# Attention values as two scaled 2-byte numbers instead of three, and the high part of the probabilities on ScalarE

## The chip, the core and the metric

The kernel runs on one NeuronCore of one Trainium2 chip. The metric is the time of one execution on the device in microseconds (us). A core has five engines that each work through a queue of their own in order: TensorE (PE, matrix products; PEld is its loading of weights), VectorE (DVE), ScalarE (ACT), GpSimd (POOL) and SyncE (SP, which here only issues DMAs). PE writes to eight PSUM banks of 128 x 512 fp32; the other operands lie in SBUF.

## The reference

One layer of an encoder on 1024 tokens of width 1024. After a normalisation, `x @ W_in` gives queries, keys and values for two attentions and two gates. Branch A is attention over a neighbourhood in a 2-D grid (8 heads, each with its own keys and values); branch B is attention over a sliding window (8 query heads that share 2 heads of keys and values). The gated branches go through `W_out`, and a SwiGLU block follows.

```python
p = jax.nn.softmax(s + bias[None], axis=-1)
o = jnp.einsum('brjhqk,brjkhd->brjqhd', p.astype(v.dtype), vg)
...
e = jnp.exp(s - m)
p = e / (jnp.sum(e, axis=-1, keepdims=True) + jnp.exp(sk - m))
o = jnp.einsum('bnkgqs,bnskd->bnqkgd', p.astype(v.dtype), vw)
...
x = x + jnp.einsum('btd,de->bte', y, w_out[l])
...
u = jax.nn.silu(jnp.einsum('btd,df->btf', h, w_gate[l])) * jnp.einsum('btd,df->btf', h, w_up[l])
x = x + jnp.einsum('btf,fd->btd', u, w_down[l])
```

All of it is fp32. On PE a product is made of parts: an fp32 operand is split into a high and a low part, and two or three matmuls stand for one product.

## The kernel before

The program has three stages: an opening (loads, splits, the projection of the first group of heads), the attention stage, and the long tail of branch products, `W_out` and the SwiGLU block. The change is in the first two.

**Groups and steps.** `order` (line 27) lists six groups: four "na" groups of two heads of branch A and two "sw" groups of four heads of branch B, in the order na 0, sw 0, na 1, sw 1, na 2, na 3. A head has eight blocks of 128 queries. One (head, block) is a step, so there are 16 steps in an na group, 32 in an sw group and 128 in all. The tiles of a group carry its number first (`o1_0_0` belongs to group 1, head 0 of it).

**One step** (`scores`, lines 679 to 710): two matmuls give the scores of 128 queries against up to 384 keys (L687, L688); DVE adds the bias and finds the bound (L693); ACT takes the exponential and its sum (L699); DVE and POOL make the scale 32768/sum (L701, L702); POOL writes the high fp16 part of the scaled probabilities `F` (L706) and DVE the low part (L707, which reads what L706 wrote); a DMA transpose on SP's queue puts both parts into `flipped` (L710). The tiles E, nm and F have 3, 4 and 3 buffers.

**Values** (`values`, lines 727 to 749) run LP = 6 steps behind the scores. A head has ten blocks: two of 128, four of 256 and four of 384 columns. The values `v` are kept as three bf16 parts of 64 columns each, and a block takes three matmuls (L745): parts 1 and 2 (128 columns of weights) with the high plane of the probabilities, the same two with the low plane, and part 3 (64 columns of weights) with the high plane. `store_half` (L718, L720) scales the finished half of a head by 1/32768.

**Projections.** While group g is in its steps, PE also works on the projection of group g+1 (`projection`, lines 252 to 481): eight tiles of 128 tokens, each 8 x 3 matmuls of 384 columns (L345) into a bank `pj` (three banks), given out in 64 pieces between the steps by `plan` (line 818). PE's order is written out by hand this way; the order on the other engines is set by a scheduler, but for the opening, where program order holds. `squares` and `scalings` normalise queries and keys (L358, L359, L363, L367, L408); `keys` and `pair` transpose them (L322, L315) and lay them out (L293, L294, L308, L309). `values_out` (lines 376 to 403) makes the three parts of the values: ACT the first (L385), DVE the rest (L399), POOL the second and third (`thirds`, L373, L374). In an sw group the values go through DRAM first, and the three parts are made at its end (`done`, L331 to L338).

**The opening.** Group 0 is projected by halves of four tiles. In the second half (`c` = 1), after k = 2, ACT squares the rows and `finish` runs for the first half. After half of k = 5 PE makes the keys' transposes (L322) into the bank `o`, of which there is one, and which until then holds tile 3 of the first half (`pj0_3`). The values of tiles 4 to 7 follow after k = 7, and then the projection of group 1.

## Time and profile before

| what | value |
|---|---|
| runs of the kernel before | 1350.4, 1354.04 and 3319.11 us (median 1354.04) |
| profiled execution, its own time | 1352.82 us |
| its span, first to last instruction | 1351.0 us |
| PE busy | 1325.9 us (98%) |
| DVE, ACT, POOL busy | 1040.8, 648.9, 257.1 us |
| L745, the matmuls of the values | 480, 101.9 us busy |
| first and last of them start at | 82.1 and 431.3 us |

The page gives the busy time of each engine, a chain of waits followed back from the last instruction, and groups of instructions with their count, their busy time, the mean duration of one, and the idle time of the engine ahead of them with what ended it. Matmuls overlap in the pipeline, so the duration of one is not what it costs; the distance from one start to the next is, and the timeline gives it. In a table by stretches, each engine's busy time stands with the count of its instructions, then PE's granted clock as a share of full speed, and the mean busy share of the 16 DMA engines.

### The profile page before, as it was taken

Reading aid. Unit: us, or ns where it says so; the run is one execution under the profiler, and the core shown is the slowest. Engines: PE = TensorE matmul, PEld = TensorE weight load, DVE = VectorE, ACT = ScalarE, POOL = GpSimd, SP = SyncE. Lnnn points to the kernel's source line nnn. Section 1 sums busy time; section 2 is a strip of 40 time slices with the busy share of each in tenths; the row PEclk is TensorE's granted clock in tenths of the full one; section 3 lists DMA queues with packets and bytes.
Section 4 is the critical chain, followed back from the end, with each engine's and each line's share of the span. In section 5 each row is a group of like instructions: output and inputs, shape, how many; then the busy total and the mean of one; then the engine's idle time right before and its main releaser. Section 6 shows DMA issues by size and latency. Waiting matters only on the chain.

```text
span 1351.0 us, 19529 instructions
## 1 busy us (share of the span) xinstructions
PE 1325.9 (98%) x6391; PEld 1085.3 (80%) x6391; DVE 1040.8 (77%) x2030; ACT 648.9 (48%) x1330; POOL 257.1 (19%) x581
## 2 busy tenths in 40 slices
...
GB/s 348 96 134 129 144 161 140 125 155 154 139 196 167 158 110 161 335 171 260 154 321 157 179 86 111 98 96 110 117 117 110 89 164 223 241 255 73 164 133 86
DMA packets 183338, 215.00 MB, mean 159 GB/s; under 512 B 110483, under 2 KB 113043, under 8 KB 183235
## 3 DMA queue, kind: packets, MB, share of 16 engines
...
## 4 chain that ended last, share of the span: by engine, by line
PE 89%; DMA 5%; DVE 2%; issue 1%; POOL 1%; ACT 1%; SPq 1%; DVEq 0%; ACTq 0%; POOLq 0%
PE pj L345 11%; PE bankZ L928 6%; PE bankZ L930 6%; PE bankZ L929 6%; PE bankY L928 6%; PE bankY L929 6%; PE bankY L930 6%; PE o L745 5%; PE bankX L928 5%; PE bankX L930 5%; PE bankX L929 5%; PE bankV L928 3%; PE bankV L929 3%; PE bankV L930 3%; PE pb L498 2%; PE pb L499 2%
## 5 line engine op out<-in xcount | busy, mean ns | idle before, releaser
L699 ACT ACTIVATE E<-E,nm 128x384 f32<-128x384 f32 (+3 forms) x128 | 75.4, 589 | 107.3 <-DVE nm L693 85.8
L745 PE MATMUL o<-flipped,v 128*128 128x256 f16 (+5 forms) x480 | 101.9, 297 | 10.2 <-DMA flipped<-F 9.0
L707 DVE SCALAR_TENSOR_TENSOR F<-E,nm,F 128x384 f16<-128x384 f32 (+1 forms) x128 | 85.7, 677 | 29.6 <-POOL F L706 29.2
L745 PEld LDWEIGHTS <-v 128*128 128x128 bf16 (+1 forms) x480 | 36.9, 101 | 72.7 <-issue 61.3
L706 POOL TENSOR_SCALAR F<-E,nm 128x384 f16<-128x384 f32 (+1 forms) x128 | 78.7, 617 | 34.8 <-DMA flipped<-F 21.0
L63 ACT CAST f<-f 128x512 fp32r<-128x512 f32 x87 | 51.7, 621 | 28.3 <-DMA f<-u_dram 27.7
L64 DVE TENSOR_TENSOR f<-f 128x512 fp32r<-128x512 f32 x87 | 56.5, 686 | 8.4 <-ACT f L63 8.2
L1334 POOL TENSOR_TENSOR rs<-rs,mhalf 128x4 f32<-128x4 f32 x2 | 2.1, 1077 | 318.0 <-DVE rs L1333 318.0
L367 POOL TENSOR_TENSOR ss<-ss,mhalf 128x4 f32<-128x4 f32 (+2 forms) x42 | 51.5, 1226 | 1.4
L693 DVE CUSTOM_DVE_ANT_0 E<-s,bna 128x384 f32<-128x384 f32 (+1 forms) x64 | 33.1, 520 | 22.6 <-PE s L688 20.0
L687 PE MATMUL s<-k,q 128*128 128x384 f32 (+1 forms) x128 | 44.4, 347 | 3.5 <-DVE nm L693 3.4
L693 DVE CUSTOM_DVE_ANT_0 E<-s,bsw,cols 128x384 f32<-128x384 f32 (+1 forms) x64 | 36.8, 577 | 6.9 <-PE s L688 5.5
L688 PE MATMUL s<-k,q 128*128 128x384 f32 (+1 forms) x128 | 41.5, 324 | 0.0
L702 POOL TENSOR_SCALAR nm<-nm 128x1 f32<-128x1 f32 x128 | 30.8, 244 | 38.9 <-DVE nm L701 33.1
L1344 ACT ACTIVATE u<-u 128x512 f32<-128x512 f32 x44 | 27.6, 630 | 19.4 <-DVE u L1343 18.8
L345 PE MATMUL pj<-wg_6h,h 128*128 128x384 f32 x96 | 33.7, 359 | 1.3 <-ACT wg_6h L63 1.3
L932 ACT COPY bankZ<-bankY 128x512 f32<-128x512 f32 x42 | 24.1, 575 | 22.3 <-PE bankY L930 22.3
L928 PE MATMUL bankY<-f,f_6h 128*128 128x512 f32 x88 | 34.4, 391 | 0.0
L929 PE MATMUL bankV<-f,f_5h 128*128 128x512 f32 x88 | 34.4, 391 | 0.0
L928 PE MATMUL bankV<-f,f_5h 128*128 128x512 f32 x88 | 34.4, 391 | 0.0
L928 PE MATMUL bankZ<-f,f_4h 128*128 128x512 f32 x88 | 34.3, 390 | 0.0
L929 PE MATMUL bankZ<-f,f_4h 128*128 128x512 f32 x88 | 34.3, 390 | 0.0
...
## 6 DMA issues: line engine op xcount, KB each, us to landing
...
```

The costliest lines, as they stand in the source:

```text
L63: a = nc.scalar.copy(hi, src)
L64: b = (eng or nc.vector).tensor_tensor(lo, src, f(hi), ALU.subtract)
L345: nc.tensor.matmul(ps[:, :384], (lh, lh, ll)[n], (his, los, his)[n][k][:, :384], start=(k == 0 and n == 0), stop=(k == 7 and n == 2))
L367: nc.gpsimd.tensor_tensor(ss, ss, mhalf[:, :n * nh], ALU.pow)
L693: att["bound"] = nc.vector.tensor_tensor_reduce(E[:, :n], s[:, :n], hd["bias"](qb), -1.0, sk if sw else 1e30, ALU.add, ALU.min, nm[:, 0:1] ...
L699: att["high"] = nc.scalar.activation(E[:, :m], E[:, :m], AF.Exp, bias=nm[:, 0:1], scale=-1.0, accum_out=nm[:, 1:2]).ins
L706: nc.gpsimd.tensor_scalar(parts[:, :, 0], blocks_of, nm[:, 1:2], 1.0, op0=ALU.mult, op1=ALU.mult)
L707: att["low"] = nc.vector.scalar_tensor_tensor(parts[:, :, 1], blocks_of, nm[:, 1:2], parts[:, :, 0], op0=ALU.mult, op1=ALU.subtract).ins
L745: nc.tensor.matmul(hd["O"][half][:rows, (a - half * 4) * P:(z + 1 - half * 4) * P], lhs, moving, start=first and i == 0, stop=last and i == 2,
L928: nc.tensor.matmul(ps, hi[:, tok(j)], bh, start=first, stop=False, skip_group_check=True)
L929: nc.tensor.matmul(ps, hi[:, tok(j)], bl, start=False, stop=False, skip_group_check=True)
L930: nc.tensor.matmul(ps, lo[:, tok(j)], bh, start=False, stop=end, skip_group_check=True)
```

## The change

The values are kept as two fp16 parts. Since fp16 has a small range, the values are first divided by a power of two for each of their columns. It comes from the length of the column of the weights that makes it.

- `column_squares`: ACT squares the high parts of the group's weights, eight blocks of 128 x 128 (na) or 128 x 64 (sw), into `sq` (L386 of the changed kernel).
- `column_norms`: PE sums them with a weight tile of ones, eight bf16 matmuls into the free columns 384 to 511 of a `pj` bank (L391); DVE writes the sums twice over (L394), halves the exponent (L396) and takes the reciprocal (L397).
- `column_scales`: PE transposes the scales of each key-value head (L403), and DVE makes a column `out_scale` of them (L404), which `store_half` uses in place of 1/32768.
- `values_out` for na: DVE multiplies the values by the reciprocal out of PSUM (L415), ACT writes the first part for both heads at once (L416), DVE the second (L417). `thirds`, POOL's part, goes. For sw, `done` has one DVE multiplication more, and POOL's two instructions go.
- `values`: two matmuls per block, both with 128 columns of weights, 320 in all for 480.
- `scores`: the high part of the probabilities is written by ACT (L743) instead of POOL, and F has four buffers instead of three.
- `load_bias`: the raw bias table moves to a shared scratch tile.

In the opening, `finish` is split: squares and scalings stay after k = 2, `column_squares` follows after k = 2 and 3, and `column_norms`, `column_scales` and the values come after k = 4. In the other groups the sums stand after tile 0 and the transposes after tile 1.

```diff
-        v = [(slot_u if kind == "na" else slot_v)(f"v{gi}_{j}").bitcast(BF16)[:, :8 * 3 * HD].rearrange(
-            "p (t a e) -> p t a e", a=3, e=HD) for j in range(nk)]
+        nv = nk * HD
+        room = (slot_u if kind == "na" else slot_v)(f"v{gi}")
+        v = room.bitcast(F16)[:, :16 * nv].rearrange("p (t j a e) -> p t j a e", j=nk, a=2, e=HD)
+        spare = slot_u(f"sq{gi}") if kind == "na" else room[:, 512:]
+        sq = spare[:, :4 * nv].bitcast(BF16).rearrange("p (k c) -> p k c", c=nv)
+        twice = spare[:, 4 * nv:6 * nv].rearrange("p (j a e) -> p j a e", j=nk, a=2)
+        wide = spare[:, 6 * nv:7 * nv].rearrange("p (j e) -> p j e", e=HD)
+        out_scale = ap.tile([P, 2], F32, tag="us", name=f"us{gi}", bufs=3)
...
-                        nc.scalar.copy(v[0][:, :, 0, :], rest)
-                        nc.vector.tensor_tensor(rest, rest, v[0][:, :, 0, :], ALU.subtract)
-                        thirds(v[0], slice(0, 8), rest)
+                        nc.vector.tensor_tensor(rest, rest, wide.to_broadcast([P, 8, HD]), ALU.mult)
+                        nc.scalar.copy(v[:, :, 0, 0], rest)
+                        nc.vector.tensor_tensor(v[:, :, 0, 1], rest, v[:, :, 0, 0], ALU.subtract)
...
-        def thirds(z, t, rest):
-
-            nc.gpsimd.tensor_copy(z[:, t, 1, :], rest)
-            nc.gpsimd.tensor_tensor(z[:, t, 2, :], rest, z[:, t, 1, :], ALU.subtract)
+        def column_squares(*which):
+
+            for k in which:
+                nc.scalar.activation(sq[:, k], f(his[k][:, nqk:384]), AF.Square, scale=gmix[:, k:k + 1])
+
+        def column_norms(ps):
+
+            for k in range(8):
+                nc.tensor.matmul(ps[:, 384:384 + nv], ones.to_broadcast([P, P]), sq[:, k],
+                                 start=k == 0, stop=k == 7, skip_group_check=True)
+            sums = ps[:, 384:384 + nv].rearrange("p (j e) -> p j e", e=HD).unsqueeze(2).to_broadcast([P, nk, 2, HD])
+            nc.vector.tensor_scalar(twice, sums, 1e-36, 1.0, op0=ALU.max, op1=ALU.mult)
+            bits = twice.bitcast(I32)
+            nc.vector.tensor_scalar(bits, bits, 1, 0x7F800000, op0=ALU.logical_shift_right, op1=ALU.bitwise_and)
+            nc.vector.reciprocal(wide, twice[:, :, 0])
+
+        def column_scales(ps):
+
+            for j in range(nk):
+                rows = twice[:, j].rearrange("p a e -> p (a e)")
+                nc.tensor.transpose(ps[:, 384:512], rows, ident)
+                nc.vector.tensor_scalar_mul(out_scale[:, j:j + 1], ps[:, 384:385], 2.0 ** -15 / VS)
...
-                rs = rows_rs[:, t:t + 1]
+                vs = ap.tile([P, 2 * HD], F32, tag="vs", name=f"vs{gi}_{t}", bufs=2)[:, :nv]
                 if kind == "na":
-                    for j in range(nk):
-                        nc.scalar.activation(v[j][:, t, 0, :], ps[:, nqk + j * HD:nqk + j * HD + HD], AF.Copy, scale=rs)
+                    vs = vs.rearrange("p (j e) -> p j e", e=HD)
+                    nc.vector.tensor_tensor(vs, ps[:, nqk:384].rearrange("p (j e) -> p j e", e=HD), wide, ALU.mult)
+                    nc.scalar.activation(v[:, t, :, 0], vs, AF.Copy, scale=rows_vs[:, t:t + 1])
+                    nc.vector.scalar_tensor_tensor(v[:, t, :, 1], vs, rows_vs[:, t:t + 1], v[:, t, :, 0],
+                                                   op0=ALU.mult, op1=ALU.subtract)
...
-            for t, ps in tiles if kind == "na" else ():
-                rest = ap.tile([P, 2 * HD], F32, tag="vs", name=f"vr{gi}_{t}", bufs=2)
-                for j in range(nk):
-                    part = rest[:, j * HD:j * HD + HD]
-                    nc.vector.scalar_tensor_tensor(part, ps[:, nqk + j * HD:nqk + j * HD + HD],
-                                                   rows_rs[:, t:t + 1], v[j][:, t, 0, :],
-                                                   op0=ALU.mult, op1=ALU.subtract)
-                    thirds(v[j], t, part)
...
                         row_norm(0)
-                        finish(list(enumerate(done)))
+                        state = squares(list(enumerate(done)))
+                        scalings(*state)
+                    if c and k == 4:
+                        column_norms(done[0])
+                        column_scales(done[1])
+                        values_out(state[0])
+                    if c and k in (2, 3):
+                        column_squares(*range(4 * k - 8, 4 * k - 4))
...
+            if not t:
+                column_squares(*range(8))
             for k in range(8):
                 multiply(ps, t, k)
+                if not t and k == 7:
+                    column_norms(ps)
+                if t == 1 and k == 7:
+                    column_scales(ps)
...
-            hd["raw"] = ap.tile([P, 384], F32, tag="braw", name=f"br{kind}{h}", bufs=1)
+            hd["raw"] = temp2(f"br{kind}{h}")[:, :384]
...
-            F = ap.tile([P, 3, 2, P], F16, tag="F", name="F" + nm_, bufs=3)
+            F = ap.tile([P, 3, 2, P], F16, tag="F", name="F" + nm_, bufs=4)
             parts = F[:, b0 - qb + 1:b1 - qb + 2]
             blocks_of = E[:, :n].rearrange("p (r c) -> p r c", c=P)
-            nc.gpsimd.tensor_scalar(parts[:, :, 0], blocks_of, nm[:, 1:2], 1.0, op0=ALU.mult, op1=ALU.mult)
+            nc.scalar.activation(parts[:, :, 0], blocks_of, AF.Copy, scale=nm[:, 1:2])
...
-                nc.scalar.activation(of[:, half_cols(half)], O, AF.Copy, scale=1 / 32768)
+                nc.scalar.activation(of[:, half_cols(half)], O, AF.Copy, scale=groups[hd["gi"]][4][:, hd["kl"]:hd["kl"] + 1])
...
-                for i, (piece, plane) in enumerate(((slice(0, 2), 0), (slice(0, 2), 1), (slice(2, 3), 0))):
-                    lhs = v[:, kb, piece].rearrange("p a e -> p (a e)")
-                    rows = lhs.shape[1]
+                lhs = v[:, kb, hd["kl"]].rearrange("p a e -> p (a e)")
+                for plane in range(2):
                     at = [(2 * qq + kb) * 256 + plane * P for qq in range(a, z + 1)]
                     moving = flipped[:, at[0]:at[-1] + P]
                     moving = bass.AP(moving.tensor, moving.offset + P - 1,
                                      [list(moving.ap[0]), [512, z + 1 - a], [-1, P]])
-                    nc.tensor.matmul(hd["O"][half][:rows, (a - half * 4) * P:(z + 1 - half * 4) * P], lhs, moving,
-                                     start=first and i == 0, stop=last and i == 2,
+                    nc.tensor.matmul(hd["O"][half][:, (a - half * 4) * P:(z + 1 - half * 4) * P], lhs, moving,
+                                     start=first and not plane, stop=last and plane == 1,
```

**Where the order moves: PE, one block of the values.** Group 0, head 0, a block of 384 columns, between pieces of the next projection (`pj`). `o` is the output bank, `v` the weights, `flipped` the transposed probabilities; the size is that of the output. Before:

```order
L345 MATMUL pj1_7_1092<-wg1_3h_529,h3_1_95 128x384
L745 LDWEIGHTS v0_0_280
L745 MATMUL o0_0_0_1075<-flipped_149,v0_0_280 128x384
L745 LDWEIGHTS v0_0_280
L745 MATMUL o0_0_0_1075<-flipped_149,v0_0_280 128x384
L745 LDWEIGHTS v0_0_280
L745 MATMUL o0_0_0_1075<-flipped_149,v0_0_280 64x384
L345 MATMUL pj1_7_1092<-wg1_4h_558,h4_1_84 128x384
```

and now:

```order
L357 MATMUL pj1_7_1101<-wg1_3h_537,h3_1_95 128x384
L781 LDWEIGHTS v0_283
L781 MATMUL o0_0_0_1086<-flipped_152,v0_283 128x384
L781 LDWEIGHTS v0_283
L781 MATMUL o0_0_0_1086<-flipped_152,v0_283 128x384
L357 MATMUL pj1_7_1101<-wg1_4h_566,h4_1_84 128x384
```

The third matmul, with an output of 64 rows, is gone with its load of weights; what stands on either side is the same.

**ACT, in the steps of group 1 (sw 0).** `E` is the exponential of a step, `F` the high part of its probabilities, `nm` the scale that F needs; `qn` and `v` belong to the projection of group 2, `of` is the output of a finished half. Before:

```order
L699 ACTIVATE E1_0_4_1568,nm1_0_4_1569<-E1_0_4_1568,nm1_0_4_1569 128x385
L358 ACTIVATE qn2_3_1612<-pj2_3_1503 128x256
L385 ACTIVATE v2_0_1201<-pj2_3_1503,rows_rs_106 128x64
L385 ACTIVATE v2_1_1202<-pj2_3_1503,rows_rs_106 128x64
L718 ACTIVATE of0_1_1533<-o0_1_1_1552 128x512
L699 ACTIVATE E1_0_5_1591,nm1_0_5_1592<-E1_0_5_1591,nm1_0_5_1592 128x385
L699 ACTIVATE E1_0_6_1634,nm1_0_6_1635<-E1_0_6_1634,nm1_0_6_1635 128x385
L699 ACTIVATE E1_0_7_1654,nm1_0_7_1655<-E1_0_7_1654,nm1_0_7_1655 128x257
L699 ACTIVATE E1_1_0_1681,nm1_1_0_1682<-E1_1_0_1681,nm1_1_0_1682 128x257
```

and now:

```order
L755 ACTIVATE of0_1_1537<-o0_1_1_1556,us0_285 128x512
L736 ACTIVATE E1_0_5_1591,nm1_0_5_1592<-E1_0_5_1591,nm1_0_5_1592 128x385
L743 ACTIVATE F1_0_4_1576<-E1_0_4_1569,nm1_0_4_1570 128x3x128
L416 ACTIVATE v2_1208<-vs2_3_1616,rows_vs_108 128x2x64
L736 ACTIVATE E1_0_6_1628,nm1_0_6_1629<-E1_0_6_1628,nm1_0_6_1629 128x385
L743 ACTIVATE F1_0_5_1598<-E1_0_5_1591,nm1_0_5_1592 128x3x128
L736 ACTIVATE E1_0_7_1648,nm1_0_7_1649<-E1_0_7_1648,nm1_0_7_1649 128x257
L743 ACTIVATE F1_0_6_1635<-E1_0_6_1628,nm1_0_6_1629 128x3x128
L743 ACTIVATE F1_0_7_1655<-E1_0_7_1648,nm1_0_7_1649 128x2x128
L736 ACTIVATE E1_1_0_1673,nm1_1_0_1674<-E1_1_0_1673,nm1_1_0_1674 128x257
```

ACT now has an F for each E. In 10 of the 128 steps F follows its own E directly; in 58 the E of another step stands between, and in 60 some other instruction.

**PE, the opening, ahead of the keys of group 0.** `tk` is the bank that `pj0_3` held, `pj0_4` and `pj0_5` are tiles of the second half. Before:

```order
L345 MATMUL pj0_4_391<-wg0_5h_207,h5_1_96 128x384
L345 MATMUL pj0_5_392<-wg0_5h_207,h5_1_96 128x384
L345 MATMUL pj0_5_392<-wg0_5l_208,h5_1_96 128x384
L345 MATMUL pj0_5_392<-wg0_5h_207,h5_1_96 128x384
L322 MATMUL tk0_0_539<-ident_74,qn0_0_439 128x128
L322 MATMUL tk0_0_539<-ident_74,qn0_1_442 128x128
```

and now (the first four rows end eight such pairs):

```order
L391 MATMUL pj0_0_290<-sq0_284,ones_109 128x128
L391 LDWEIGHTS ones_109
L391 MATMUL pj0_0_290<-sq0_284,ones_109 128x128
L403 MATMUL pj0_1_291<-ident_74,sq0_284 128x128 x2
...
L357 MATMUL pj0_4_395<-wg0_5h_210,h5_1_96 128x384
L357 MATMUL pj0_5_396<-wg0_5l_211,h5_1_96 128x384
L357 MATMUL pj0_5_396<-wg0_5h_210,h5_1_96 128x384
L334 MATMUL tk0_0_547<-ident_74,qn0_0_444 128x128
L334 MATMUL tk0_0_547<-ident_74,qn0_1_447 128x128
```

The sums and two transposes stand ahead of the keys. `tk` can be written when DVE has read `pj0_3` for the last time. Before, that reading was the fourth L408, behind the eight L399 of the values. Now the four L408 come first, and the last reading is the fourth L415, which stands behind L394 to L397 (they read PE's sums), both L404 (they read PE's transposes) and three rounds of L415 and L417, each with ACT's L416 between.

## The prediction

> **What bounds the kernel now.** I read the page first, for the engine that is busy and for the chain of waits.

> ```profile
> PE 1325.9 (98%) x6391; PEld 1085.3 (80%) x6391; DVE 1040.8 (77%) x2030; ACT 648.9 (48%) x1330; POOL 257.1 (19%) x581
> ...
> PE 89%; DMA 5%; DVE 2%; issue 1%; POOL 1%; ACT 1%; SPq 1%; DVEq 0%; ACTq 0%; POOLq 0%
> ...
> L745 PE MATMUL o<-flipped,v 128*128 128x256 f16 (+5 forms) x480 | 101.9, 297 | 10.2 <-DMA flipped<-F 9.0
> ```

> PE is busy for 98% of the span and is 89% of the chain that ended last. So time on PE is time of the kernel, as long as the other engines keep up. The third row is what the change cuts: 480 matmuls, 101.9 us. Then I read the table by stretches, cut where a group's steps begin (na 0, sw 0, na 1, sw 1, na 2, na 3), and the same table for the second score matmul alone.

> ```profile
> core 0: us, PE busy (x) PEld busy (x) DVE busy (x) ACT busy (x) POOL busy (x), PEclk, DMA share, GB/s
> 60.00:112.00 52.00, 50.67 (x287) 43.94 (x286) 39.67 (x100) 28.93 (x73) 35.01 (x65) 0.98 0.59 122
> 112.00:188.00 76.00, 71.47 (x389) 52.20 (x388) 59.24 (x168) 40.16 (x110) 54.47 (x139) 1.00 0.79 148
> 188.00:245.00 57.00, 55.82 (x313) 45.16 (x312) 38.45 (x100) 28.81 (x73) 36.22 (x69) 1.00 0.67 136
> 245.00:320.00 75.00, 70.17 (x372) 51.51 (x372) 55.83 (x164) 38.45 (x108) 51.70 (x139) 0.98 0.79 150
> 320.00:377.00 57.00, 57.00 (x310) 44.81 (x309) 37.40 (x110) 29.39 (x76) 35.02 (x80) 1.00 0.70 145
> 377.00:432.00 55.00, 50.66 (x220) 30.27 (x219) 38.36 (x94) 22.63 (x55) 21.30 (x39) 0.94 0.78 168
> ```

> ```profile
> 112.00:188.00 76.00, 10.26 (x32) 5.88 (x32) 1.00 0.79 148
> ```

> One L688 is one step, so sw 0 has 32 of them in 76 us, as the code says. In na 0, na 1 and na 2 PE is busy for 163.5 of 166 us (98%), and a step takes 166/48 = 3.46 us. In the two sw groups it is 141.6 of 151 us (94%); a step takes 151/64 = 2.36 us, of which PE works 2.21, DVE (59.24 + 55.83)/64 = 1.80, ACT 78.61/64 = 1.23, and the DMA engines 0.79 x 2.36 = 1.86. I call those 64 steps and the 16 of na 3 the short ones. They hold little work of projections, so the other engines are nearer to PE there.

> **The matmuls of the values.** What a matmul costs is the distance to the next start. The timeline of PE shows a block of each width, and projections between them.

> ```profile
> 189.60 0.78 PE L745 MATMUL o<-flipped,v 128*128 128x384 f16 x3
> 190.31 0.44 PE L345 MATMUL pj<-wg_7h,h 128*128 128x384 f32 x1
> ...
> 192.33 0.33 PE L345 MATMUL pj<-wg_2h,h 128*128 128x384 f32 x1
> 192.50 0.33 PE L345 MATMUL pj<-wg_2l,h 128*128 128x384 f32 x1
> ...
> 193.37 0.62 PE L745 MATMUL o<-flipped,v 128*128 128x256 f16 x3
> 193.92 0.44 PE L345 MATMUL pj<-wg_4h,h 128*128 128x384 f32 x1
> ...
> 196.47 0.46 PE L745 MATMUL o<-flipped,v 128*128 128x128 f16 x3
> 196.86 0.44 PE L345 MATMUL pj<-wg_0h,h 128*128 128x384 f32 x1
> ...
> 199.92 1.72 PE L745 MATMUL o<-flipped,v 128*128 128x128 f16 x9
> 201.57 0.44 PE L345 MATMUL pj<-wg_5h,h 128*128 128x384 f32 x1
> ```

> A block of 384 columns takes 190.31 - 189.60 = 0.71 us, one of 256 takes 0.55, one of 128 takes 0.39. The last two rows are three blocks in a row (128, 256, 384): 1.65 us, which is the sum of the three. A projection's matmul of 384 columns takes only 0.17. So three matmuls without any wait would take 0.52, and a block holds 0.19 more. Where it lies, the loading of weights shows in another block of 384:

> ```profile
> 204.57 0.12 PEld L745 LDWEIGHTS <-v 128*128 128x128 bf16 x2 [0.16 <-issue]
> 205.01 0.11 PEld L745 LDWEIGHTS <-v 128*64 128x64 bf16 x1 [0.32 <-issue]
> 205.29 0.19 PEld L345 LDWEIGHTS pj<-wg_1h,h 128*128 128x128 f32 x1 [0.17 <-issue]
> ```

> The first two loads start together; that of 64 columns starts 0.44 later, where two matmuls would have been done after 0.35; and PE is 0.28 further before the next load, where 0.17 is the matmul. So the third piece brings waits of 0.09 ahead of it and 0.11 behind it besides its own 0.17. Since the three blocks in a row have the same waits at their borders, where fp16 work follows fp16 work, I put both down to the load of 64 columns and not to the change of type. From 0.39, 0.55 and 0.71, each matmul adds 0.16/3 = 0.053 us per 128 columns, which makes 0.067, 0.12 and 0.174 for one matmul of 128, 256 and 384 columns.

> A head now costs 2 x 0.39 + 4 x 0.55 + 4 x 0.71 = 5.82 us. Two matmuls per block without waits cost 2 x 0.134 + 4 x 0.24 + 4 x 0.348 = 2.62. That saves 3.20 us a head, **0.40 us a step and 51.2 us in all**. If the wait of 0.11 belongs to leaving fp16 work after all, it stays in 160 blocks and 17 us less are saved: 34 us, a third of 101.9. I take 51, by the row of the three blocks.

> [...]

> **What PE gets in addition.** Per group eight matmuls of 64 or 128 columns (L391) and one or two transposes (L403). At 0.067 the 48 matmuls cost 3.2 us; if each exposed its load, 0.11 as in the load rows above, 5.3. Ten transposes at 0.63/4 = 0.16, from the first row of the next fence, cost 1.6. I take **+4.8 us**, 3 to 7.

> PE also waits for what they read. For the opening, PE's two longest waits there stand in its timeline, and DVE's prices in the groups by shape:

> ```profile
> 35.66 0.63 PE L322 MATMUL tk<-ident,qn 128*128 128x128 f32 x4 [0.79 <-DVE qn L408]
> ...
> 55.54 1.44 PE L322 MATMUL tk<-ident,qn 128*128 128x128 f32 x4 [3.18 <-ACT qn L358]
> ```

> ```profile
> L399 DVE SCALAR_TENSOR_TENSOR vr<-pj,rows_rs,v 128x64 f32<-128x64 f32 x64 | 15.0, 276 | 8.7 <-POOL v L374 7.4 <-POOL ss L365 1.1
> L408 DVE TENSOR_TENSOR qn<-pj,ss 128x256 f32<-128x256 f32 x32 | 12.9, 419 | 3.8 <-POOL ss L367 3.7
> ```

> The keys' transposes now wait for DVE's fourth L415, since `tk` takes the bank of `pj0_3`. Ahead of it on DVE, once PE's sums are done: L394 and L396 on 256 columns, 0.42 each by L408; L397, not in the trace, between one column and 256, say 0.3; two short L404, 0.3; then three rounds of L415, ACT's L416 and L417, at about 0.33 each, between 276 ns for 64 columns and 419 for 256, which makes 3.0; and the last L415, 0.33: 4.8 us. PE does its two transposes and six matmuls meanwhile, 1.4 us, and waits 3.4 where it now waits 0.79. That is +2.6 us, and I add 0.2 for what is queued behind on DVE (the splits of group 1's weights, then its keys): **+2.8 us**, 1 to 5. The second wait, 3.18 us, ends on ACT's squares of group 1, behind POOL's parts of the values. POOL's part goes, and eight squares of weights on ACT (0.3 each, 2.4 us) and four more rounds take its place ahead of PE's sums. I count no change, -3 to +3.

> In groups 2 to 5 the squares of the weights stand on ACT among the steps, and PE's sums come one tile later. In na 0 and na 1 the last two squares stand behind the E of a step whose scores PE does some 2.2 us ahead of the sums; score to E takes ACT some 3 us, so PE waits 0.8 there: **+1.6 us**, 0 to 6.

> **What moves between the other engines.** These rows are the step's own chain and the parts of the values on ACT.

> ```profile
> L699 ACT ACTIVATE E<-E,nm 128x384 f32<-128x384 f32 (+3 forms) x128 | 75.4, 589 | 107.3 <-DVE nm L693 85.8
> ...
> L707 DVE SCALAR_TENSOR_TENSOR F<-E,nm,F 128x384 f16<-128x384 f32 (+1 forms) x128 | 85.7, 677 | 29.6 <-POOL F L706 29.2
> ...
> L706 POOL TENSOR_SCALAR F<-E,nm 128x384 f16<-128x384 f32 (+1 forms) x128 | 78.7, 617 | 34.8 <-DMA flipped<-F 21.0
> ...
> L702 POOL TENSOR_SCALAR nm<-nm 128x1 f32<-128x1 f32 x128 | 30.8, 244 | 38.9 <-DVE nm L701 33.1
> ```

> ```profile
> POOL F L706 <- DMA flipped<-F: 21.0, 16, 2.7
> ```

> ```profile
> L385 ACT ACTIVATE v<-pj,rows_rs 128x64 bf16<-128x64 f32 x64 | 16.2, 316 | 1.2 <-POOL rows_rs L169 1.1
> ...
> L358 ACT ACTIVATE qn<-pj 128x256 f32<-128x256 f32 x32 | 11.5, 380 | 9.8 <-PE pj L345 9.5
> ```

> POOL loses F (78.7 us) and its parts of the values, and with them a wait of 21 us for a free F buffer, of which there are now four. ACT gets F, 128 times between 0.38 (256 columns) and 0.59 us (E): 0.55. The parts of the values are one L416 in place of two L385, which pays for the squares. So in a short step ACT works 1.78 us, DVE 1.80 and 0.04 for the new small instructions, the DMA engines 1.86, and PE 2.21 - 0.40 = 1.81. No engine has room any more: PE at its 94% of today would give 1.93 us, no gain at all 2.36. The chain that hangs on them has five to six steps of slack, and it loses POOL's waits, so I go a third of the way from the lower end: 2.07.

> Another row speaks for the lower end: L707 reads what POOL used to write, beside it.

> ```profile
> L707 DVE SCALAR_TENSOR_TENSOR F<-E,nm,F x128: 466/615/1410, 66.9 to 422.9; 128x384 f16<-128x384 f32 x96, 128x256 f16<-128x256 f32 x32
> ```

> Its duration runs from 466 to 1410 ns for the same two shapes; without POOL's F at the same time part of that spread should go. [...]

> **The sum.** Long steps: 48 x 0.40 = -19.2 us, since PE is at 98% there and ACT at (28.93 + 28.81 + 29.39)/48 + 0.55 = 2.37 of 3.06 us stays under it. Steps of sw: 64 x (2.36 - 2.07) = -18.6. na 3, where PE is idle for 4.3 of 55 us: two thirds of 6.4, -4.2. With +4.8, +2.8 and +1.6 this is -32.8 us. The profiled execution took 1352.8 us, 1.8 more than its span and 1.2 less than the median of the runs, so no correction is needed: **1320 us**. The tail after 432 us is not touched by the change and stays as it is.

> **The rivals.**
> - PE stays the only bound. Then all of the 51.2 us comes: 1352.8 - 51.2 + 9.2 = 1311 us. For it: the 98% of the long steps, POOL's relief. Against: three other resources at 1.78 to 1.86 us of a short step.
> - The chain of a step sets the short steps. Six steps of lag must cover scores, E, F, the low part and the transpose; F now queues on ACT behind other work. Then the short steps keep their 2.36 us: 1352.8 - 19.2 + 9.2 = 1343 us. For it: the same loads; the DMA engines at 0.79 already. Against: the wait for F's buffer that goes.
> - ACT stalls at F, and the kernel is slower than before. F can't start before POOL's nm (L702), and whatever stands behind F on ACT waits too: the next E, and the squares that PE's sums need. POOL idles 34.8 us before F and 38.9 before nm now, 0.58 us a step together. If ACT takes over a wait of w, a short step is 1.78 + w: above w = 0.58 the short steps lose, and above 0.70 the loss over 80 of them, 80 x 0.12, eats the rest of the gain. At w = 0.9: 80 x 0.32 = +25.6, long steps 2.37 + 0.9 = 3.27 instead of 3.46, -9.1, and +9.2: 1378 us. Against: in 118 of 128 steps something else stands between a step's E and its F.

> **How the numbers follow.** The forecast has 0.58 (its own range is 1311 to 1331), PE alone 0.15, the chain 0.20, ACT 0.07. The range from 1305 to 1348 holds the first three but for their tails; the 17 us of the exit wait (1337) lie in it too. A measurement of this kernel can tell about 2%, 27 us, from no change, so the border is 1327. Faster: 0.15 and four fifths of 0.58, 0.61. Same: 0.12, the chain's 0.20 and a little of ACT's, 0.34. Slower: 0.05.

> **What would show it.** Right: 320 matmuls of the values with distances of 0.07, 0.12 and 0.17 and no wait after a block; long steps of about 3.06 us and sw steps of 2.0 to 2.15; one wait of some 3 us at the keys in the opening; F of about 0.55 us on ACT. Wrong: a wait of 0.11 behind each block; sw steps still near 2.36 with PE waiting for `flipped`; ACT idle ahead of F for more than half a microsecond a step, with PE waiting for score banks.

## The result, and the profile after

The changed kernel takes 1335.95 us in the median of four runs (1332.92 to 1339.86), the kernel before 1352.22. The ratio is 0.9887, with a 95% interval from 0.9840 to 0.9933: 1.1% or 16 us faster, where 33 were forecast. The median lies inside the predicted range of 1305 to 1348 us, but above the 1327 from which a clear gain was to count. One of the executions of the kernel before took 3319.11 us; the ratio leaves it out. The profiled execution of the changed kernel took 1332.92 us, 19.9 less than that of before.

The page of the changed kernel, its engines and its group of the values' matmuls:

```profile
PE 1278.9 (96%) x6289; PEld 1083.9 (81%) x6289; DVE 1043.7 (78%) x2060; ACT 720.7 (54%) x1474; POOL 146.6 (11%) x324
...
L781 PE MATMUL o<-flipped,v 128*128 128x256 f16 (+2 forms) x320 | 62.6, 294 | 22.6 <-DMA flipped<-F 18.7
```

PE's share falls from 98 to 96%, and the wait of the values for the flipped probabilities grows from 9.0 to 18.7 us. The table by stretches says where. It has seven stretches, cut at the first L688 or L725 of each group: opening, na 0, sw 0, na 1, sw 1, na 2, and na 3 with the last values behind its scores. They end with the last matmul of the values (431.3 and 410.5 us). First the kernel before, then the changed one.

```profile
0.00:60.70 60.70, 55.38 (x295) 53.28 (x296) 37.02 (x84) 38.41 (x83) 21.28 (x53) 0.95 0.70 241
60.70:112.00 51.30, 49.98 (x284) 43.24 (x283) 39.67 (x100) 28.93 (x73) 34.95 (x64) 0.99 0.59 122
112.00:188.40 76.40, 71.87 (x391) 52.60 (x390) 59.64 (x168) 40.16 (x110) 54.87 (x140) 1.00 0.79 148
188.40:245.50 57.10, 55.92 (x314) 45.26 (x313) 38.05 (x100) 28.89 (x73) 36.32 (x68) 1.00 0.68 137
245.50:323.40 77.90, 73.07 (x388) 53.43 (x387) 59.05 (x173) 40.22 (x112) 53.55 (x143) 0.98 0.79 151
323.40:377.70 54.30, 54.30 (x295) 42.68 (x294) 34.86 (x102) 27.62 (x70) 33.37 (x78) 1.00 0.68 143
377.70:431.30 53.60, 49.26 (x215) 29.45 (x214) 36.99 (x91) 22.15 (x53) 20.60 (x38) 0.94 0.79 171
sum 431.30, PE 409.77 PEld 319.92 DVE 305.27 ACT 226.38 POOL 254.94; mean PE 58.54 PEld 45.70 DVE 43.61 ACT 32.34 POOL 36.42
```

```profile
core 0: us, PE busy (x) PEld busy (x) DVE busy (x) ACT busy (x) POOL busy (x), PEclk, DMA share, GB/s
0.00:69.90 69.90, 58.48 (x314) 55.55 (x315) 40.08 (x92) 42.17 (x91) 13.10 (x24) 0.93 0.61 210
69.90:119.20 49.30, 45.82 (x282) 42.65 (x281) 40.67 (x105) 37.59 (x93) 21.14 (x37) 1.00 0.60 126
119.20:190.20 71.00, 61.97 (x360) 53.76 (x359) 56.69 (x173) 55.99 (x143) 30.49 (x83) 0.93 0.81 161
190.20:242.90 52.70, 49.48 (x303) 44.55 (x302) 40.85 (x108) 39.43 (x99) 25.13 (x43) 1.00 0.70 149
242.90:312.70 69.80, 59.29 (x358) 51.55 (x357) 58.86 (x178) 57.24 (x145) 30.38 (x83) 0.98 0.87 170
312.70:360.80 48.10, 46.79 (x275) 41.35 (x274) 35.83 (x102) 34.15 (x78) 16.48 (x34) 1.00 0.71 151
360.80:410.50 49.70, 40.25 (x187) 28.86 (x186) 35.55 (x92) 31.48 (x73) 7.78 (x21) 0.91 0.81 189
sum 410.50, PE 362.08 PEld 318.27 DVE 308.52 ACT 298.06 POOL 144.50; mean PE 51.73 PEld 45.47 DVE 44.07 ACT 42.58 POOL 20.64
```

PE's work fell by 409.8 - 362.1 = 47.7 us, close to the 46.4 of the forecast (51.2 less 4.8). But PE was idle for 21.5 us before and is for 48.4 now. So more than half of the saving went into waits. By stages:

| stage | before | after | change | forecast |
|---|---|---|---|---|
| opening | 60.7 | 69.9 | +9.2 | +2.8 |
| na 0, na 1, na 2 | 162.7 | 150.1 | -12.6 | -19.2 and +1.6 |
| sw 0, sw 1 | 154.3 | 140.8 | -13.5 | -18.6 |
| na 3 and the last values | 53.6 | 49.7 | -3.9 | -4.2 |
| the rest | 919.7 | 920.6 | +0.9 | 0 |

(The forecast had 4.8 more for PE's new work, spread over the first three rows.) Of the opening's 9.2 us, 6.1 are idle time of PE (69.90 - 58.48 against 60.70 - 55.38), and 3.1 are busy time: the new matmuls, and one more stretch at half clock, as shown below.

Single waits of PE in the timeline of the changed kernel, four in the opening and two in the steps:

```profile
34.40 0.33 PE L403 MATMUL pj<-ident,sq 128*128 128x128 f32 x1 [0.85 <-DVE sq L396]
35.41 0.33 PE L403 MATMUL pj<-ident,sq 128*128 128x128 f32 x1 [0.68 <-DVE us L404]
...
39.42 1.09 PE L334 MATMUL tk<-ident,qn 128*128 128x128 f32 x4 [2.63 <-DVE vs L415]
...
57.12 1.89 PE L391 MATMUL pj<-v,ones 128*128 128x64 bf16 x8 [5.68 <-ACT v L386]
```

```profile
237.66 0.33 PE L403 MATMUL pj<-ident,sq 128*128 128x128 f32 x1 [2.07 <-DVE us L404]
...
309.56 0.33 PE L403 MATMUL pj<-ident,sq 128*128 128x128 f32 x1 [2.38 <-DVE us L404]
```

The second transpose of a pair waits until DVE has read the first, since both go into the same PSUM columns. That reading stands in DVE's queue among the work of the steps. The table of waits has the sum:

```profile
PE pj L403 <- DVE us L404: 6.5, 4, 2.4
```

And PE's granted clock, in stretches of 3.41 us from 36.00 and from 53.07:

```profile
36.00:39.41 3.41, 0.79 (x5) 0.49 (x4) 1.79 (x7) 1.30 (x4) 0.00 (x0) 1.00 0.77 221
39.41:42.83 3.42, 3.40 (x12) 3.42 (x13) 2.46 (x6) 3.37 (x8) 0.00 (x0) 0.50 0.50 150
42.83:46.24 3.41, 3.41 (x22) 3.38 (x22) 2.55 (x4) 2.37 (x4) 0.00 (x0) 1.00 0.90 258
53.07:56.48 3.41, 0.00 (x0) 0.00 (x0) 1.86 (x7) 1.25 (x4) 3.12 (x2) 1.00 0.00 0
56.48:59.90 3.42, 2.58 (x11) 1.83 (x11) 2.07 (x6) 2.79 (x11) 0.00 (x0) 0.50 0.12 18
59.90:63.31 3.41, 3.41 (x12) 3.41 (x12) 2.44 (x7) 0.12 (x1) 1.44 (x2) 0.50 0.16 50
```

Behind a stretch in which PE was mostly idle (0.79 and 0.00 us busy), the next stretch runs at half clock, and, where PE is busy throughout, it does 12 matmuls in it instead of 22. Such a stretch costs half its length, 1.7 us. From 20 us to the last matmul of the values there are five of them before (8.5 us) and ten after (17.0 us). A wait of PE that empties enough of such a stretch thus costs more than its own length.

### The profile page after: what moved, and what is told of

It is laid out like the page before. It is cut to its first block, busy times and chain, and to the rows that moved or that the text cites. A ratio compares the mean times of both kernels' runs of the same rounds, so it can differ in the third digit from the quotient of the medians.

```text
span 1331.1 us, 19107 instructions
## 1 busy us (share of the span) xinstructions
PE 1278.9 (96%) x6289; PEld 1083.9 (81%) x6289; DVE 1043.7 (78%) x2060; ACT 720.7 (54%) x1474; POOL 146.6 (11%) x324
## 4 chain that ended last, share of the span: by engine, by line
PE 72%; DMA 2%; DVE 1%; issue 0%; SPq 0%; ACT 0%; DVEq 0%; ACTq 0%
PE bankZ L964 6%; PE bankZ L965 6%; PE bankZ L966 6%; PE bankY L964 6%; PE bankY L965 6%; PE bankY L966 6%; PE bankX L966 5%; PE bankX L965 4%; PE bankX L964 4%; PE bankV L965 3%; PE bankV L964 3%; PE bankV L966 3%; PE pb L537 2%; PE pb L536 2%; PE pb L535 2%; PE pj L357 2%
## 5 line engine op out<-in xcount | busy, mean ns | idle before, releaser
L744 DVE SCALAR_TENSOR_TENSOR F<-E,nm,F 128x384 f16<-128x384 f32 (+1 forms) x128 | 79.3, 627 | 16.8 <-ACT F L743 16.0
L743 ACT ACTIVATE F<-E,nm 128x384 f16<-128x384 f32 (+1 forms) x128 | 73.9, 583 | 24.4 <-POOL nm L739 17.3
L781 PE MATMUL o<-flipped,v 128*128 128x256 f16 (+2 forms) x320 | 62.6, 294 | 22.6 <-DMA flipped<-F 18.7
L736 ACT ACTIVATE E<-E,nm 128x384 f32<-128x384 f32 (+3 forms) x128 | 74.7, 584 | 17.6 <-DVE nm L730 13.3
L781 PEld LDWEIGHTS <-v 128*128 128x128 f16 x320 | 23.0, 100 | 45.8 <-issue 42.3
L725 PE MATMUL s<-k,q 128*128 128x384 f32 (+1 forms) x128 | 42.2, 329 | 0.0
L730 DVE CUSTOM_DVE_ANT_0 E<-s,bsw,cols 128x384 f32<-128x384 f32 (+1 forms) x64 | 37.1, 579 | 5.9 <-PE s L725 4.6
L739 POOL TENSOR_SCALAR nm<-nm 128x1 f32<-128x1 f32 x128 | 29.7, 233 | 101.4 <-DVE nm L738 96.1
L730 DVE CUSTOM_DVE_ANT_0 E<-s,bna 128x384 f32<-128x384 f32 (+1 forms) x64 | 33.1, 517 | 8.3 <-PE s L725 7.2
L357 PE MATMUL pj<-wg_4h,h 128*128 128x384 f32 x96 | 33.7, 361 | 1.6 <-ACT wg_4h L65 1.6
L964 PE MATMUL bankZ<-f,f_7h 128*128 128x512 f32 x88 | 34.4, 390 | 0.0
L964 PE MATMUL bankZ<-f,f_4h 128*128 128x512 f32 x88 | 34.3, 390 | 0.0
```

The costliest lines, as they stand in the source:

```text
L357: nc.tensor.matmul(ps[:, :384], (lh, lh, ll)[n], (his, los, his)[n][k][:, :384], start=(k == 0 and n == 0), stop=(k == 7 and n == 2))
L730: att["bound"] = nc.vector.tensor_tensor_reduce(E[:, :n], s[:, :n], hd["bias"](qb), -1.0, sk if sw else 1e30, ALU.add, ALU.min, nm[:, 0:1] ...
L736: att["high"] = nc.scalar.activation(E[:, :m], E[:, :m], AF.Exp, bias=nm[:, 0:1], scale=-1.0, accum_out=nm[:, 1:2]).ins
L743: nc.scalar.activation(parts[:, :, 0], blocks_of, AF.Copy, scale=nm[:, 1:2])
L744: att["low"] = nc.vector.scalar_tensor_tensor(parts[:, :, 1], blocks_of, nm[:, 1:2], parts[:, :, 0], op0=ALU.mult, op1=ALU.subtract).ins
L781: nc.tensor.matmul(hd["O"][half][:, (a - half * 4) * P:(z + 1 - half * 4) * P], lhs, moving, start=first and not plane, stop=last and plan ...
```

## The experiments

Theory 1: PE waits for the making of the scales. Theory 2: F on ACT, and with it the chain of a step, sets the pace. Theory 3: F on ACT is a gain. Theory 4, from the second set on: the DMA transposes and F's buffers set the short steps. Each ratio is to the kernel before on the same chip, whose median was 1351.6 to 1353.1 us. A difference to the changed kernel (1335.95 us) is uncertain by some 6 us, since its own interval is the widest, and one between two other kernels by 2 to 4 us.

**The scales as constants** (their matmuls, squares and readings left out).

```diff
-                nc.scalar.activation(sq[:, k], f(his[k][:, nqk:384]), AF.Square, scale=gmix[:, k:k + 1])
...
+            nc.vector.memset(wide, 1.0)
...
+            nc.vector.memset(out_scale, 2.0 ** -15)
```

> The changed kernel with the column scales as constants: ACT's squares of the weights, PE's sums (L391) and transposes (L403) and DVE's work on them are left out; the multiplication by a reciprocal, now 1, stays. Theory 1 (the gain was lost in PE's waits for the making of the scales): PE loses 5.6 us of work (3.7 and 1.9), 6.5 us of waits between the two transposes of a pair, 0.85 us ahead of the first, about 1 of the 2.6 us at the keys and 1 to 2 of the 5.9 us ahead of group 1's sums, with one stretch of half clock (1.7 us) or two: 16 to 19 us under the changed kernel, 1317 to 1320. Theory 2 (F on ACT and the step's chain set the pace in the attention stage, so that what PE saves elsewhere comes back as waits for the flipped probabilities): only the opening's part comes, 4 to 8 us, 1328 to 1332.

1319.7 us, ratio 0.9765 [0.9749, 0.9781], 16.2 us under the changed kernel. Theory 1 holds for this part: making the scales costs 16 us, of which PE's own work is 5.6.

**One reading for a pair of scales.**

```diff
-                nc.tensor.transpose(ps[:, 384:512], rows, ident)
-                nc.vector.tensor_scalar_mul(out_scale[:, j:j + 1], ps[:, 384:385], 2.0 ** -15 / VS)
+                nc.tensor.matmul(ps[:, 384 + j:385 + j], rows, ident[:, :1], start=True, stop=True, skip_group_check=True)
+            nc.vector.tensor_scalar_mul(out_scale[:, :nk], ps[:, 384:384 + nk], 2.0 ** -15 / VS)
```

> The changed kernel with the column scales brought into a column by a matmul with the first column of the identity, each into a PSUM column of its own, and one reading by DVE for both: the second of a pair no longer waits for DVE to have read the first. Theory 1: 6.5 us of PE's waits go (0.7, 1.3, 2.1, 2.4), and about 1 us of work; 5 to 8 us under the changed kernel, 1328 to 1331. Theory 2: the two waits that lie in na groups' projections among sw steps come back as waits for the flipped probabilities: 1 to 3 us under it.

1328.4 us, ratio 0.9827 [0.9810, 0.9844], 7.6 us under the changed kernel, as theory 1 asks: about the 6.5 us of the wait and 1 us of work. The interval is too wide to say that the wait comes back in full.

**F's high part on POOL in the changed kernel, and on ACT in the kernel before.** The same line both ways:

```diff
-            nc.scalar.activation(parts[:, :, 0], blocks_of, AF.Copy, scale=nm[:, 1:2])
+            nc.gpsimd.tensor_scalar(parts[:, :, 0], blocks_of, nm[:, 1:2], 1.0, op0=ALU.mult, op1=ALU.mult)
```

> The changed kernel with F's high part back on POOL; F keeps four buffers. Theory 1: ACT's part in the waits is small; within 5 us of the changed kernel, 1331 to 1341. Theory 2 (F on ACT delays E and the flipped probabilities, so POOL would be better): 6 to 15 us under it, 1321 to 1330. Theory 3 (F on ACT is worth a lot, since POOL's F took 0.6 us of the chain and slowed DVE's low part beside it): 6 to 15 us over it, 1342 to 1351, with DVE's low part back to 0.68 us from 0.63.

> The kernel before with one line changed: F's high part is written by ACT instead of POOL (three buffers of F, three parts of the values as before). Theory 1: PE stays at 98% in the long steps; the sw steps and na 3, where PE waited 9 us for the flipped probabilities, get back up to a half: 0 to 5 us under the kernel before. Theory 2: ACT's queue delays E and the low part; 3 to 15 us slower than before. Theory 3: all of the 9 us of waits and the half clocks behind them go: 8 to 14 us faster.

On POOL in the changed kernel: 1326.3 us, ratio 0.9808 [0.9795, 0.9821], 9.7 us under it; theory 2. On ACT in the kernel before: 1342.9 us, 0.9932 [0.9920, 0.9945], 9.3 us faster; theory 3. The same edit has opposite signs in the two kernels, so neither theory is the whole. The groups of ACT and DVE, first of the changed kernel, then of the one with F on POOL:

```profile
L744 DVE SCALAR_TENSOR_TENSOR F<-E,nm,F 128x384 f16<-128x384 f32 (+1 forms) x128 | 79.3, 627 | 16.8 <-ACT F L743 16.0
L743 ACT ACTIVATE F<-E,nm 128x384 f16<-128x384 f32 (+1 forms) x128 | 73.9, 583 | 24.4 <-POOL nm L739 17.3
...
L736 ACT ACTIVATE E<-E,nm 128x384 f32<-128x384 f32 (+3 forms) x128 | 74.7, 584 | 17.6 <-DVE nm L730 13.3
```

```profile
L744 DVE SCALAR_TENSOR_TENSOR F<-E,nm,F 128x384 f16<-128x384 f32 (+1 forms) x128 | 84.0, 662 | 17.9 <-POOL F L743 16.8
L743 POOL TENSOR_SCALAR F<-E,nm 128x384 f16<-128x384 f32 (+1 forms) x128 | 77.4, 606 | 15.0 <-DMA flipped<-F 5.8 <-ACT E L736 0.9 <-ACT of L757 0.4
L736 ACT ACTIVATE E<-E,nm 128x384 f32<-128x384 f32 (+3 forms) x128 | 75.2, 588 | 77.1 <-DVE nm L730 54.6 <-POOL E L734 6.3 <-POOL nm L739 5.4
```

With F on POOL, ACT has 77 us of idle time ahead of the exponentials, so they start when their bound is there. With F on ACT it has 18, and the mean distance from L730 to the exponential is 1.63 and 1.48 us in sw 0 and sw 1 instead of 1.13 and 0.97.

**The order in the opening, and later sums in the sw groups.**

```diff
+            ahead = scaled(*tiles[0])
...
+                    if i + 1 < len(tiles):
+                        ahead = scaled(*tiles[i + 1])
                     nc.scalar.activation(v[:, t, :, 0], vs, AF.Copy, scale=rows_vs[:, t:t + 1])
...
-            if not t:
+            if t == (2 if kind == "sw" else 0):
                 column_squares(*range(8))
...
-                if not t and k == 7:
+                if t == (3 if kind == "sw" else 0) and k == 7:
...
-                if t == 1 and k == 7:
+                if t == (4 if kind == "sw" else 1) and k == 7:
```

> The changed kernel with two edits of order. In the values of several tiles DVE multiplies the next tile (L415) ahead of the low part of this one (L417), so that ACT's L416 lies beside it; and in the sw groups the squares, the sums and the transpose of the scales come two and three tiles later (they are needed at the group's end only). Theory 1: PE's wait at the keys falls from 2.6 to about 1 us, that of 5.9 us ahead of group 1's sums to 0 to 3, and one or two of the three stretches of half clock in the opening go (1.7 us each): the first scores come 5 to 9 us earlier than at 69.9 us, and the time is 5 to 9 us under the changed kernel. Theory 2 (the opening is bound by DVE and ACT, PE waits for the second half's keys instead): 0 to 3 us under it.

1323.5 us, ratio 0.9792 [0.9779, 0.9805], 12.4 us under the changed kernel, more than expected. The run makes both edits at once, so their shares are not known. The first scores come at 60.0 us instead of 69.9. In the opening the wait ahead of the sums is gone, that at the keys is halved, and one half-clock stretch is left of three:

```profile
38.43 1.09 PE L334 MATMUL tk<-ident,qn 128*128 128x128 f32 x4 [1.30 <-DVE vs L415]
```

**All three** (one reading, F on POOL, the orders).

> The changed kernel with all three: the scales by one-column matmuls with one reading, F's high part back on POOL, and the two edits of order in the opening. If the three losses are waits at separate places (theory 1), their sum comes: 7.6 + 9.7 + 5 to 9, 22 to 26 us under the changed kernel, 1309 to 1314. If they cover one another (the attention stage takes its pace from the chain of a step whatever PE saves, theory 2): 12 to 17 us under it, 1319 to 1324.

1313.8 us, ratio 0.9716 [0.9696, 0.9735]: 22.2 us under the changed kernel and the fastest of the kernels that leave nothing out. The three repairs are worth 7.6 + 9.7 + 12.4 = 29.7 by themselves and 22.2 together: at separate places, with some overlap.

**A third matmul per block again, with 64 and with 128 columns of weights** (`P` in place of `HD` in its list for 128; the third matmul counts the high plane twice, so these two kernels serve for their time alone).

```diff
-                for plane in range(2):
+                for i, (rows, plane) in enumerate(((P, 0), (P, 1), (HD, 0))):
...
-                    nc.tensor.matmul(hd["O"][half][:, (a - half * 4) * P:(z + 1 - half * 4) * P], lhs, moving,
+                    nc.tensor.matmul(hd["O"][half][:rows, (a - half * 4) * P:(z + 1 - half * 4) * P], lhs[:, :rows], moving,
```

> The changed kernel with a third matmul per block, as the kernel before had: the first 64 columns of the same weights with the high plane again (so the sum counts that part twice). It is looked at for the cost of a block alone: the distance from its first matmul to the second projection matmul behind it, less one projection matmul, now 0.18, 0.24 and 0.34 us for 128, 256 and 384 columns. The prediction's reading (the load of 64 columns brings waits of 0.09 and 0.11): +0.26, +0.31, +0.36. If a third piece costs its stream alone: +0.07, +0.12, +0.17. If it was the mixed types (bf16 weights, fp16 data) that cost, the same +0.07 to +0.17.

> As the one with 64 columns, but the third matmul has all 128 columns of the weights (so the high plane counts twice). The prediction's reading: no waits, +0.07, +0.12 and +0.17 per block, 0.2 less than with 64 columns. If any third matmul costs more than its stream, the same as with 64 columns.

PE's timeline at the same block, with two matmuls (the changed kernel), with a third of 64 columns, and with a third of 128:

```profile
93.90 0.50 PE L781 MATMUL o<-flipped,v 128*128 128x384 f16 x2
94.10 0.47 PE L357 MATMUL pj<-wg_4h,h 128*128 128x384 f32 x1
94.41 0.34 PE L357 MATMUL pj<-wg_4l,h 128*128 128x384 f32 x1
```

```profile
94.98 0.78 PE L781 MATMUL o<-flipped,v 128*128 128x384 f16 x3
95.69 0.44 PE L357 MATMUL pj<-wg_4h,h 128*128 128x384 f32 x1
95.97 0.34 PE L357 MATMUL pj<-wg_4l,h 128*128 128x384 f32 x1
```

```profile
94.30 0.66 PE L781 MATMUL o<-flipped,v 128*128 128x384 f16 x3
94.66 0.47 PE L357 MATMUL pj<-wg_4h,h 128*128 128x384 f32 x1
94.97 0.34 PE L357 MATMUL pj<-wg_4l,h 128*128 128x384 f32 x1
```

From the block's start to the second projection matmul behind it: 0.51, 0.99 and 0.67 us. The third of 64 columns costs 0.48, that of 128 only 0.16; for blocks of 256 columns the medians are 0.42 and 0.11, for 128 columns 0.32 and 0.06 (17 and 13 blocks between projections). So the piece of 64 columns brings 0.26 to 0.32 us of waits. The type of the weights doesn't matter: with fp16 throughout, a block costs the 0.99 us that it cost before with bf16 weights. The whole kernels took 1359.9 and 1343.9 us, by one run each.

**Values 5 steps behind instead of 6**, on the kernel with all three repairs.

```diff
-        LP = 6
+        LP = 5
```

> The kernel with all three repairs (1313.8 us), with the values 5 steps behind the scores instead of 6. Theory 2 (latency: scores, E, F, low part and transpose must fit into the lag): the short steps, 2.1 to 2.2 us now, get longer by up to a fifth, 80 x 0.15 to 0.35, 12 to 28 us over it, 1326 to 1342. Theory 4 (throughput of an engine or of the DMA queues sets the short steps, the lag is long enough): 0 to 4 us over it.

1323.9 us, ratio 0.9800 [0.9777, 0.9824], 10.2 us over it: less than theory 2 asks, more than theory 4 allows. A step of lag is 2.1 us of slack, and it is worth 10 us. Seven steps were not tried.

**Four buffers of F in the kernel before** (with the raw bias table in the shared scratch tile, as in the change)**; three in the changed kernel with F on POOL.**

```diff
-            F = ap.tile([P, 3, 2, P], F16, tag="F", name="F" + nm_, bufs=3)
+            F = ap.tile([P, 3, 2, P], F16, tag="F", name="F" + nm_, bufs=4)
```

> The kernel before with four buffers of F instead of three (and the raw bias table in the shared scratch tile, as the change has it); F's high part stays on POOL, three parts of the values. If the 21 us for which POOL waited ahead of F for a free buffer were what F's move to ACT cured in the kernel before (9.3 us there): 4 to 9 us faster than before, 1343 to 1348. If it was POOL's own load (parts of the values, 21.9 and 17.4 us, beside F): 0 to 3 us faster.

> The changed kernel with F's high part on POOL, as the one that took 1326.3 us, but with three buffers of F instead of four. If the buffers matter: 4 to 10 us over it, 1330 to 1336. If it is POOL's load that counts, which the change has taken away with the parts of the values: within 3 us of it, 1323 to 1329.

Before, with four: 1341.2 us, 0.9916 [0.9902, 0.9931], 11.9 us faster. Changed, F on POOL, with three: 1338.0 us, 0.9891 [0.9871, 0.9911], 11.8 us slower than with four. Both are more than was expected of the buffer. POOL's F in the kernel before with four buffers:

```profile
L706 POOL TENSOR_SCALAR F<-E,nm 128x384 f16<-128x384 f32 (+1 forms) x128 | 77.6, 608 | 11.8 <-DMA flipped<-F 5.5
```

Its wait for a free buffer is 5.5 us instead of 21.0. So in the kernel before F's move to ACT, worth 9.3 us, seems to have made up for the missing buffer; the run with F on ACT and three buffers, below, bears this out.

**Only the high part transposed** (the low plane stays zero, so the product with the low part is left out; F's two planes lie one behind the other for it), on the kernel with all three repairs.

```diff
-            nc.sync.dma_start(turned.rearrange("p (r c) -> p r c", c=P), parts.rearrange("p r a c -> p (r a c)"), transpose=True)
+            nc.sync.dma_start(turned.rearrange("p (r a c) -> p r a c", a=2, c=P)[:, :, 0], F[:, 0, b0 - qb + 1:b1 - qb + 2].rearrange("p r c -> p (r c)"), transpose=True)
```

> The kernel with all three repairs (1313.8 us), but the DMA transpose carries the high part of the probabilities alone; the low plane stays zero, so the product with the low parts is left out of the result (its matmuls run on zeros, and DVE still writes the low parts). Theory 4, with the DMA queues as the bound (their busy share is 0.8 to 0.87 in the short steps): steps near PE's 1.95 us, 8 to 16 us under it, 1298 to 1306. Theory 2 (latency): the transpose's 1.2 us get shorter by a third or so, 2 to 5 us under it. If neither DMA nor the chain behind it counts: within 2 us.

1303.0 us, ratio 0.9633 [0.9610, 0.9655], 10.7 us under it. sw 0 and sw 1 with all three repairs, and here:

```profile
107.20:174.80 67.60, 58.67 (x352) 51.29 (x351) 57.23 (x172) 42.09 (x115) 49.52 (x118) 0.97 0.90 166
...
225.70:296.50 70.80, 61.14 (x361) 53.38 (x360) 58.83 (x179) 42.88 (x114) 49.37 (x117) 0.95 0.90 170
```

```profile
110.10:174.30 64.20, 58.52 (x351) 51.34 (x350) 57.42 (x172) 41.96 (x113) 48.73 (x116) 0.97 0.57 128
...
225.10:291.30 66.20, 58.70 (x360) 51.49 (x360) 58.05 (x175) 41.51 (x110) 47.88 (x116) 0.97 0.64 136
```

The DMA engines' share falls from 0.90 to 0.57 and 0.64, and PE's idle time from 8.9 and 9.7 us a group to 5.7 and 7.5. But the transpose no longer waits for DVE's low part either: the mean from the scores to its issue falls by 0.9 us. So this run shows that the way through the transpose holds the short steps up, and not whether its volume or its delay does. A third reading was not tried: SP's own time. Issuing one transpose occupies SP for 1.23 us in the median with all repairs, and for 1.19 with half the data, where a third less was expected:

```profile
L755 SPq DMA_TRANSPOSE flipped<-F x128: 1188/1226/2711, 66.4 to 385.2; - x128
...
L756 SPq DMA_TRANSPOSE flipped<-F x128: 1168/1192/2598, 67.0 to 372.8; - x128
```

With the other DMAs, issuing takes 73 and 70% of SP's time in sw 0 and sw 1 of the kernel before, 78 and 79% in the changed kernel, and 84 and 81% here. The mean time from the end of DVE's low part to the issue of its transpose is 0.40 and 0.44 us before, 0.92 and 0.71 in the changed kernel. The page does not count issuing as busy time, and the prediction's loads of a short step do not have it.

**The third matmul alone taken out of the kernel before** (the third part of the values is still made, but left out of the product)**; the same with four buffers of F.**

```diff
-                for i, (piece, plane) in enumerate(((slice(0, 2), 0), (slice(0, 2), 1), (slice(2, 3), 0))):
+                for i, (piece, plane) in enumerate(((slice(0, 2), 0), (slice(0, 2), 1))):
```

> The kernel before with the third matmul of each block taken out (the third part of the values is still made, but left out of the result); F stays on POOL with three buffers, nothing is added. The prediction's sum for this part alone, 19.2 + 18.6 + 4.2: 42 us faster than before, 1310. Theory 4 (outside the long steps PE's time is worth little, since F's buffers and the transposes set the pace): the long steps give 48 x 0.4 to 0.55, the others 0 to 8: 20 to 32 us faster, 1320 to 1332. PE as the only bound: 62 us, 1290.

> As the one with two matmuls, with four buffers of F (and the raw bias table in the shared scratch tile). The buffer was worth 11.9 us with three matmuls and 11.8 us in the changed kernel with F on POOL. If it is worth as much whatever PE does: 10 to 14 us under the one with three buffers. If it is the very thing that kept PE's saving from coming through: 15 to 25 us under it.

1324.7 us, 0.9791 [0.9771, 0.9811], 27.3 us faster: theory 4's range, not the 42 of the forecast. With four buffers 1318.6 us, 0.9753 [0.9733, 0.9773], only 6.1 us less, less than either guess: the buffer and the saving on PE cover each other in part.

**F on ACT with three buffers, and F on ACT in the repaired kernel** (the two diffs above).

> The changed kernel with three buffers of F instead of four; F's high part stays on ACT. If the buffer is worth the same with F on ACT as on POOL (11.8 us): 8 to 14 us over the changed kernel, 1344 to 1350. If F on ACT and the fourth buffer cure the same wait (each alone was worth 9 and 12 us in the kernel before): within 3 us of it, 1333 to 1339.

> The kernel with all three repairs (1313.8 us), but with F's high part on ACT again. If F on ACT costs the same here as in the changed kernel (9.7 us): 1321 to 1326. If it cost there because ACT also had the squares of the weights and the values' first parts at the wrong time, which the edits of order have moved: within 4 us, 1312 to 1318.

With three buffers 1337.6 us, 0.9898 [0.9880, 0.9916], 1.6 us over the changed kernel, which is within the noise. So with F on ACT no worth of the fourth buffer shows, with F on POOL it was 11.8 us: they cure the same wait. In the repaired kernel F on ACT costs 4.2 us (1318.0 us, 0.9750 [0.9732, 0.9768]) where it cost 9.7 in the changed one. The intervals of these two prices overlap, so it is not shown that a part of the price hung on the other losses.

**The factor 32768 on DVE instead of POOL**, in the changed kernel and in the one with all repairs.

```diff
-            nc.gpsimd.tensor_scalar(nm[:, 1:2], nm[:, 1:2], 32768.0, 1.0, op0=ALU.mult, op1=ALU.mult)
+            nc.vector.tensor_scalar(nm[:, 1:2], nm[:, 1:2], 32768.0, 1.0, op0=ALU.mult, op1=ALU.mult)
```

> The changed kernel with the multiplication by 32768 (L739) on DVE, right behind the reciprocal, instead of POOL; F's high part stays on ACT. If ACT's price of 9.7 us is the time that it stands ahead of F for POOL's nm (17.3 us by the groups) with E behind it: a hop from engine to engine goes, the stall falls by a third to two thirds, and the time is 3 to 8 us under the changed kernel, 1328 to 1333. If it is F's own 0.58 us in ACT's queue ahead of the next E: within 2 us, 1334 to 1338.

> The kernel with all three repairs (1313.8 us; F's high part on POOL) with the multiplication by 32768 on DVE as well. The chain of a step loses a hop of some 0.3 us; with the lag worth 10 us for a step of it (2.1 us), that is 1 to 2 us under it; if POOL's time ahead of F matters more, up to 5 us under it, 1309 to 1313; if DVE, busy for 85% of a short step, gets in the way: up to 3 us over it.

1340.4 us, 0.9913 [0.9894, 0.9932], and 1323.5 us, 0.9783 [0.9764, 0.9801]: 4.5 and 9.7 us slower, where a gain or no change was expected. The first lies within the noise, the second is clear of it. Groups of ACT and DVE in the first:

```profile
L736 ACT ACTIVATE E<-E,nm 128x384 f32<-128x384 f32 (+3 forms) x128 | 75.0, 586 | 36.9 <-DVE nm L730 22.3 <-DVE nm L739 7.3 <-DVE nm L738 5.2
L743 ACT ACTIVATE F<-E,nm 128x384 f16<-128x384 f32 (+1 forms) x128 | 72.8, 580 | 15.8 <-DMA flipped<-F 4.7 <-ACT E L736 3.5 <-DVE nm L739 2.6
...
L739 DVE TENSOR_SCALAR nm<-nm 128x1 f32<-128x1 f32 x128 | 19.0, 149 | 1.7
```

ACT's stall ahead of F did fall, from 24.4 to 15.8 us, but that ahead of the exponentials rose from 17.6 to 36.9: DVE is late with the bounds. In the repaired kernel 128 short instructions more on DVE (0.15 us each in the rows above) cost more than the hop to POOL that they save.

## Why the prediction went wrong, step by step

The runs make a ladder from the kernel before to the changed one:

| step | measured | forecast |
|---|---|---|
| third matmul out | -27.3 | -42.0 (with the next row) |
| fourth buffer of F | -6.1 | |
| two scaled parts with their bound for three parts | +7.6 | +9.2 |
| F's high part from POOL to ACT | +9.7 | 0 |
| sum | -16.1 | -32.8 |

(1352.1, 1324.7, 1318.6, 1326.3 and 1336.0 us. By the intervals the first three rows are uncertain by 3 to 4 us each, the last by 6.5.)

- **The matmuls of the values: right in kind, mis-sized.** 0.40 us a step was forecast, from waits of 0.09 and 0.11 around the load of 64 columns. The runs with a third matmul give 0.26 to 0.32 us of waits, and the net time of these matmuls on PE (starts to starts, less idle time) fell from 94.2 to 32.2 us, 62 instead of 51. The prediction counted a block up to the first projection matmul behind it, 0.71 us for 384 columns. Counted to the second, less one projection matmul, it is 0.99 - 0.17 = 0.82. The rival reading, a wait on leaving fp16, fell: in the changed kernel the block takes 0.51 - 0.17 = 0.34 us, two matmuls of 0.17 and no wait behind them. In the two runs with a third matmul 64 columns of weights cost more than 128, 0.48 us against 0.16 at the same block. Why a load of 64 columns brings a wait is not shown by any run.
- **The long steps: close.** Of 19.2 us, the third matmul alone brings 16.2 in the profile (na 0 to 2: 162.7 to 146.5 us), and the changed kernel 12.6: in it 1.34 and 2.07 us go to the second transposes in na 0 and na 1.
- **The short steps: this step failed.** I put them "a third of the way from the lower end", at 2.07 us; they take 140.8/64 = 2.20, between the forecast and the rival in which a step's chain leaves them as they were. The 2.36 that I started from is too short as well: the stretches were cut at round numbers, and from first scores to first scores it is 154.3/64 = 2.41 (and 162.7/48 = 3.39 for 3.46 in the long steps). With the third matmul alone gone, the sw steps take 145.3/64 = 2.27, a gain of 0.14 where 0.29 was forecast. The loads of a step came out as worked out (DVE 1.81, ACT 1.77, PE 1.89 us); that the slack of five to six steps would cover the chain did not. In the repaired kernel one step less of lag costs 10 us, and halving the transpose brings 11. Whether the delay of the chain, the volume of the transposes or SP's time for issuing them holds these steps up stays open.
- **F on ACT: this step failed too.** It was costed at nothing, covered by ACT's idle time, with the fourth buffer and POOL's relief put down to it. F took 0.58 us as forecast (0.55), and the stall ahead of it is 24.4/128 = 0.19 us, far from the 0.58 at which the third rival was to decide. But it has a price, 9.7 us in the changed kernel and 4.2 in the repaired one, and the gain that it was to bring is the buffer's. ACT's idle time ahead of the exponentials is 18 us with F on ACT and 77 with F on POOL, so they queue behind F. That this is what costs the time is not shown: taking POOL out of the chain ahead of F cut ACT's stall there and made the kernel no faster.
- **What PE gets in addition: the work right, its waits missed.** The sums and transposes cost 3.7 and 1.9 us for 4.8. The wait between two transposes of a pair was not seen, 6.5 us; the order of DVE's queue showed it, L404 between two L403. The wait at the keys was forecast at 3.4 us and is 2.63, with 0.85 and 0.68 ahead of the two transposes. The wait at 55.54 us was to stay as it was; in its place PE waits 5.68 us at 57.12, for ACT's squares of the weights, instead of 3.18. The making of the scales costs 16 us in all. So the opening took 9.2 us more and not 2.8, the largest miss of any stage. That the third row of the ladder is only 7.6 I put down to POOL's parts of the values, which went; this was not tried alone.
- **The half clock was left out of every term.** The rows of the prediction had the granted clock in them (0.98, 0.94), and it was not read. Twice as many half-clock stretches are 8.5 us.
